# Output projection in seven block products: last sums made on chip, one operand split earlier, evictions and transposes in another order

## The chip, the core and the metric

The kernel runs on one core of a Trainium2 chip. Five engines work side by side, each through its own queue in order: TensorE (PE, with its weight loads shown apart as PEld), VectorE (DVE), ScalarE (ACT), GpSimd (POOL) and SyncE (SP), which issues the transfers. They meet at semaphores. The metric is the device time of one execution in microseconds; before the change the median of three runs is 1611.94 us (1611.52 to 1611.96).

## What is computed

One decoder block on a sequence of 1024 rows of 1024 features, all in float32. The part that matters here lies between the two branches and the feed-forward layer:

```python
branch_a = (jax.nn.silu(rg) * ry) @ w_ret_out[l]
branch_b = ay.reshape(B, S, ATTN_Q) @ w_attn_out[l]
merged = jax.nn.sigmoid(gate_a) * branch_a + jax.nn.sigmoid(gate_b) * branch_b
x = x + merged @ w_out[l]
h2 = rms_norm(x, ln2_g[l])
x = x + (jax.nn.silu(h2 @ w_ffn_gate[l]) * (h2 @ w_ffn_up[l])) @ w_ffn_down[l]
return rms_norm(x, lnf_g)
```

## The kernel before

**Numbers in two parts.** A float32 operand is split into a high part (a cast on ACT) and a low part (a subtraction on DVE); a product is three matmuls: high by high, high by low, low by high. `halves`, `wsplit` and `sum_halves` (L1301) make such pairs.

**Seven products.** The output projection `merged @ w_out` is cut into two by two blocks of 512 and done with seven block products, P1 to P7, in place of eight (Strassen's scheme in Winograd's form). `merged` is kept transposed; its blocks are a11, a21 (first and second half of the sequence, features 0 to 511) and a12, a22 (features 512 to 1023), those of w_out b11, b12, b21, b22. P1 takes a11 and b11, P2 a12 and b21. The others take sums: on the left S1 = a21 + a22 (P5), S2 = S1 - a11 (P6), a12 - S2 (P3), S3 = a11 - a21 (P7) and a22 alone (P4); on the right b12 - b11 (P5), t2 = b22 - (b12 - b11) (P6), b22 (P3), b22 - b12 (P7) and b21 - t2 (P4). Each product is 4 x 4 x 3 = 48 matmuls: four k of 128 features, four row tiles tt, three pairs.

**Branch A** (the loop over n, L1099) multiplies 128 features of branch A at a time, in the order 0, 4, 1, 5, 2, 6, 3, 7, each in two halves of the sequence of 24 matmuls, into three accumulator banks in turn. `evac` adds branch B and splits a11, a12 and a22 into m0 and m1. After each second n, k = n - 4 has all four blocks, and POOL makes the four sums of that k in place (L1120 to L1126) and SP writes them to DRAM (`ms_d`). From there P5's, P6's and P7's sums are read back whole (`load_sum`, L1296), then cast and subtracted (`sum_halves`).

**Tiles.** m0 and m1 hold four operand parts each; the tiles `wob` (b12, b22, t2) and `sA` (operands of P5 and P6) take the space of branch A's input, which its last product frees. x2 is the residual; it takes the space of branch A's temporaries, so its loads (`load_x`, L1299) wait for the last write to DRAM. `xf` and `a1` later take the space of `wob` and `sA`. P1, P6, P7 and P4 add up in the four banks `vbank`, P2, then P5 and P3 in the four banks `obank`, which have the names s and t.

**Order.** From L1366 DVE, ACT and PE are held to the written order (`in_order`); POOL's and SP's order is the scheduler's. `by_k` runs a product k by k over all row tiles, `by_t` one row tile with all k. `gain` (L1351) adds a bank into x2. The written order is P2, P1, P5, P6 by k, then P3 by row tile, then for each row tile of the second half P7 and P4, each followed by its `gain`. For each block t of 128 rows, `ln2_a` squares x2 and sums it (ACT, L1358), POOL makes the reciprocal root (L98, L100), `ln2_b` scales (ACT, L1362), and `columns` (L1224) transposes the result in eight matmuls and multiplies by the gain vector (L1237). For the first half `columns` also splits it into `a1` for the feed-forward products; for the second half it makes the Strassen sums (L1246 to L1248, on POOL for t below 6, else on DVE), which `s2_part` and `a22_part` split into m0 and m1. There are two tiles `hx` for the scaled blocks. `prep_to` splits feed-forward weights, `early_t` makes their sums.

## Time and profile before

| what | us |
|---|---|
| median of three runs | 1611.94 |
| the profiled execution | 1604.04 |
| its span, first to last instruction | 1602.2 |
| PE busy in the span | 1563.7 |
| DVE, ACT, POOL busy | 1020.0, 730.7, 406.4 |
| branch A's last matmul group ends, P2 starts | 850.73 |
| first feed-forward matmul starts | 965.90 |

Times inside the span count from its start. In the timeline a row merges instructions that follow each other without a gap: start, length, engine, line, operation, output<-inputs, count, and in brackets how long the engine had stood idle before and what ended that. Matmuls are pipelined, so their listed lengths overlap; the distance from start to start is what one takes.

### The profile page before, as it was taken

To read this page: it belongs to the slowest core of one execution; us is meant where nothing else is said; L and a number is where in the kernel's file an instruction comes from. 1 tells how busy PE (TensorE), PEld (TensorE's weight loads), DVE (VectorE), ACT (ScalarE), POOL (GpSimd) and SP (SyncE) were. 2 spreads that over 40 slices of the span, in tenths; PEclk is the share of its full clock that TensorE was granted. 3 is DMA by queue.
4 is the path that set the end of the run, shared out by engine and by line. 5 is a ranking of instruction groups with operands and counts; after the bars stand their busy time and mean duration, and the time that the engine had idled before them with its cause. 6 is when DMAs were issued, how large, how long until landed. Compare 5 with 4: busy or idle time off the path is not lost.

```text
span 1602.2 us, 20889 instructions
## 1 busy us (share of the span) xinstructions
PE 1563.7 (98%) x7435; PEld 1298.7 (81%) x7435; DVE 1020.0 (64%) x1792; ACT 730.7 (46%) x1456; POOL 406.4 (25%) x333
## 2 busy tenths in 40 slices
PE   9999999999999999999998969999999999999998
PEld 8887788888888888888886748888888888888886
DVE  6469987778566654887555658444444444578756
...
GB/s 210 167 155 145 178 216 165 108 138 39 186 171 152 132 158 238 209 195 113 219 184 259 93 1 59 99 106 99 106 105 108 114 100 102 277 258 92 99 99 125
DMA packets 154230, 231.51 MB, mean 144 GB/s; under 512 B 9420, under 2 KB 81934, under 8 KB 152591
## 3 DMA queue, kind: packets, MB, share of 16 engines
...
q8 instruction: 58, 0.95, 0.2%
q14 instruction: 46, 0.37, 0.1%
q10 hardware_dynamic: 2, 0.00, 0.0%
...
## 4 chain that ended last, share of the span: by engine, by line
PE 83%; ACT 6%; DVE 4%; issue 2%; DMA 2%; POOL 1%; SPq 0%; POOLq 0%; DVEq 0%; ACTq 0%
PE fA L1474 15%; PE fB L1474 7%; PE dA L1753 7%; PE wA L842 6%; PE dxP L1753 6%; PE fC L1474 4%; PE wB L842 3%; PE va L687 3%; PE acc_g L158 2%; PE acc_g L159 2%; PE acc_g L160 2%; PE vP L687 2%; ACT sc L467 2%; PE acc_bb L158 2%; PE acc_bb L159 2%
## 5 line engine op out<-in xcount | busy, mean ns | idle before, releaser
L1753 PE MATMUL dA<-dwP,daP 128*128 128x512 f32 x528 | 120.6, 389 | 0.0
L1753 PEld LDWEIGHTS dA<-dwP,daP 128*128 128x128 f32 x528 | 99.0, 188 | 20.7 <-DVE dwP L134 0.2
L1753 PE MATMUL dxP<-dwP,daP 128*128 128x512 f32 x396 | 90.2, 389 | 0.0
L1753 PEld LDWEIGHTS dxP<-dwP,daP 128*128 128x128 f32 x396 | 74.3, 188 | 15.4
L452 POOL COPY sc<-nsink 128x4 f32<-128x4 f32 x32 | 13.1, 412 | 274.4 <-PE pT L485 157.1
L158 PE MATMUL acc_g<-h,wh_g 128*128 128x512 f32 x192 | 75.5, 393 | 0.1
L159 PE MATMUL acc_g<-h,wh_g 128*128 128x512 f32 x192 | 75.2, 392 | 0.0
L160 PE MATMUL acc_g<-h,wl_g 128*128 128x512 f32 x192 | 75.1, 393 | 0.0
L467 ACT ACTIVATE sc<-sc,nm 128x257 f32<-128x257 f32 (+1 forms) x128 | 62.5, 492 | 27.1 <-DVE nm L464 26.7
L1543 POOL TENSOR_TENSOR xf<-xf 128x512 f32<-128x512 f32 x40 | 60.3, 1507 | 30.4 <-issue 28.8
L1485 POOL TENSOR_TENSOR xf<-xf 128x512 f32<-128x512 f32 x33 | 49.8, 1510 | 55.0 <-ACT t_1P L131 23.1
L464 DVE CUSTOM_DVE_ANT_0 sc<-s,amask,nsink 128x256 f32<-128x256 f32 (+1 forms) x128 | 54.2, 463 | 9.8 <-PE s L461 9.5
L1495 ACT COPY xf<-fA 128x512 f32<-128x512 f32 x44 | 25.7, 586 | 74.1 <-PE fA L1474 74.1
L1658 POOL TENSOR_TENSOR rs_f<-tot,mhalf 128x1 f32<-128x1 f32 x8 | 4.8, 605 | 205.4 <-DVE tot L1655 205.4
L134 DVE TENSOR_TENSOR dwP<-wd,dwP 128x512 fp32r<-128x512 f32 x77 | 52.9, 687 | 5.4 <-ACT dwP L131 5.4
L556 POOL TENSOR_TENSOR wr_wp<-wr_wp 128x512 f32<-128x512 f32 x10 | 16.6, 1657 | 140.0 <-DVE w0P L134 122.5
L131 ACT CAST dwP<-wd 128x512 fp32r<-128x512 f32 x77 | 47.4, 616 | 9.3 <-PE dA L1753 7.1
L158 PE MATMUL acc_bb<-ay,wh_bb 128*128 128x512 f32 x128 | 51.0, 400 | 0.0
L131 ACT CAST daP<-daP 128x512 fp32r<-128x512 f32 x42 | 26.0, 620 | 54.1 <-PE dxP L1753 26.7
L159 PE MATMUL acc_bb<-ay,wh_bb 128*128 128x512 f32 x128 | 50.3, 393 | 0.0
L160 PE MATMUL aq<-h,wl_aq 128*128 128x512 f32 x128 | 50.2, 392 | 0.0
L158 PE MATMUL aq<-h,wh_aq 128*128 128x512 f32 x128 | 50.2, 392 | 0.0
...
## 6 DMA issues: line engine op xcount, KB each, us to landing
...
daP<-act_d SPq DMA_DIRECT2D x21, 512.0 KB, 10.5
...
```

The source lines that it names most:

```text
L131: nc.scalar.copy(hi, raw)
L134: return nc.vector.tensor_tensor(out=lo, in0=raw, in1=f32(hi), op=ALU.subtract)
L158: nc.tensor.matmul(pt, hi[:, k, :], xh, start=(k == 0), stop=False)
L159: nc.tensor.matmul(pt, hi[:, k, :], xl, start=False, stop=False)
L160: nc.tensor.matmul(pt, lo[:, k, :], xh, start=False, stop=(k == 7))
L464: nc.vector.tensor_tensor_reduce(out=sc[:, j, 0:nk], in0=pt[:, jj * 256:jj * 256 + nk], in1=mk, scale=1.0, scalar=nsink[:, 4 * g + j:4 * g ...
L467: nc.scalar.activation(sc[:, j, 0:nk + 1], sc[:, j, 0:nk + 1], AF.Exp, scale=-1.0, bias=nm[:, j:j + 1], accum_out=den[:, j:j + 1])
L687: nc.tensor.matmul(vbanks[pr][tt], x_[:, c], w[:, u, :], start=(fresh and k + z == 0), stop=(k == 3 and z == 2), skip_group_check=not fresh)
L842: nc.tensor.matmul(pt, o[:, w, k, :], v, start=(first and k + z == 0), stop=(k == 3 and z == 2), skip_group_check=not first)
L1474: nc.tensor.matmul(pt, o[:, w, k, :], v, start=(first and k + z == 0), stop=(k == 3 and z == 2), skip_group_check=not first)
L1543: nc.gpsimd.tensor_tensor(out=o, in0=a, in1=b, op=op)
L1753: nc.tensor.matmul(banks[tt], a[:, u, c], w[:, v, :], start=(fresh and f + z == 0), stop=(f == NP - 1 and z == 2), skip_group_check=not fresh)
```

## The change

1. In branch A, for k = 0, 1, 2, S3 (P7's operand) is split into m1 at once (`halves`) and not written to DRAM.
2. For k = 3 the four sums are made on DVE, and ACT and DVE split three of them straight into `sA` and m1. Only P3's sum (a12) is written. `sA` is loaded for k below 3 only, and these loads and those of `wob` are issued ahead of it.
3. The helpers and the loads of b11 and b21 stand earlier in the text, and the written order on DVE and ACT begins there.
4. P5's weights are split ahead of the `gain` of P2, P6's sums and weights ahead of the `gain` of P1; t2 takes the place of b21 for P4, made on POOL after P6's split. `load(1)` comes before P3's weights.
5. Of the first half's blocks only two are squared and scaled inside P3. Then `c22(tt)` (P7 of a row tile and its `gain`) and `c21(tt)` (P4 and its `gain`) alternate with the columns: c22(0), c22(1), c21(0), c22(2), c21(1), c22(3), c21(2), c21(3). Column 6 comes between the first two feed-forward products, column 7 behind them.
6. `columns` no longer splits the first half; `hi_part` (ACT) and `lo_part` (DVE) do it later. S2's last two parts and all four of a22's stand behind column 7, and the transposes take s and t banks by turns.

```diff
-            if kh:
+            if kh and k < 3:
                 a11, a21, a12, a22 = (parts.pop(i) for i in ((0, 0), (0, 1), (1, 0), (1, 1)))
                 nc.gpsimd.tensor_tensor(out=a22, in0=a21, in1=a22, op=ALU.add)
                 nc.sync.dma_start(ms_d[0, k], a22)
                 nc.gpsimd.tensor_tensor(out=a21, in0=a11, in1=a21, op=ALU.subtract)
-                nc.sync.dma_start(ms_d[2, k], a21)
+                halves(a21, m1[:, 0, k, :], m1[:, 1, k, :])
...
+        for y in range(2):
+            nc.sync.dma_start(wob[:, 4 * y:4 * y + 4], blk(y, 1))
+            nc.sync.dma_start(f32(sA[:, 2 * y + 1, 0:3]), ms_d[y, 0:3].rearrange("k p t -> p k t"))
+
+        late = in_order(nc.vector.engine, nc.scalar.engine)
+        late.__enter__()
+        a11, a21, a12, a22 = (parts.pop(i) for i in ((0, 0), (0, 1), (1, 0), (1, 1)))
+        v_ = nc.vector.tensor_tensor
+        v_(out=a22, in0=a21, in1=a22, op=ALU.add)
+        v_(out=a21, in0=a11, in1=a21, op=ALU.subtract)
+        nc.scalar.copy(sA[:, 0, 3], a22)
+        v_(out=a11, in0=a22, in1=a11, op=ALU.subtract)
+        nc.scalar.copy(m1[:, 0, 3], a21)
+        v_(out=a12, in0=a12, in1=a11, op=ALU.subtract)
+        nc.scalar.copy(sA[:, 2, 3], a11)
+        nc.sync.dma_start(ms_d[2, 3], a12)
+        for hl, q, src in ((sA, 0, a22), (m1, 0, a21), (sA, 2, a11)):
+            v_(out=hl[:, q + 1, 3], in0=src, in1=f32(hl[:, q, 3]), op=ALU.subtract)
...
-            pt = ps("s", 2, f"h2T{t}{q}")
+            pt = ps("ts"[t % 2], 2, f"h2T{t}{q}")
...
     sub2(nc.vector, b11, b12, b11)
-    sum_halves("P5")
-    sum_halves("P7")
+    sum_halves("P5", 3)
     by_k("P2")
 
-    for tt in range(4):
-        gain(0, tt, 0, obank["P2"][tt])
     W["P5"] = slots4(("tw", "tw"), "P5")
     wsplit(b11, W["P5"])
     sub2(nc.gpsimd, t2, b22, b11)
+    for tt in range(4):
+        gain(0, tt, 0, obank["P2"][tt])
...
     for tt in range(4):
         by_t("P3", tt)
+        if 0 < tt < 3:
+            ln2_b(tt - 1)
         gain(0, tt, 1, obank["P5"][tt])
-        ln2_a(tt)
-        if tt > 1:
-            columns(tt - 2)
-        ln2_b(tt)
-    early_t(0, 2)
-    for tt in range(4):
-        t = 4 + tt
+        if tt < 2:
+            ln2_a(tt)
+        if tt == 2:
+            early_t(0, 2)
+
+    def c21(tt):
+        by_t("P4", tt)
+        gain(1, tt, 0, vbank[tt])
+
+    def c22(tt):
         by_t("P7", tt)
         gain(1, tt, 1, vbank[tt])
...
+    c22(3)
+    ln2_b(5)
+    columns(4)
+    prep_to(4)
+    c21(2)
+    ln2_a(6)
+    columns(5)
+    ln2_b(6)
+    c21(3)
+    ln2_a(7)
+    s2_part(4)
+    ln2_b(7)
```

Three places show how instructions move. The first is on DVE, from the end of branch A to P2's evictions. `woP1..` and `woP5..` are the weight halves of P1 and P5, `wr_b110` and `wrx_b111` the two halves of b11, `ms..` the four blocks of k = 3. Before:

```order
L1271 TENSOR_TENSOR woP111_8225<-wrx_b111_8206,woP110_8224 128x1024
L560 TENSOR_TENSOR m1_7577<-ms11_8181,m1_7577 128x512
L1275 TENSOR_TENSOR wr_b110_8205<-wob_8230,wr_b110_8205 128x1024
L1275 TENSOR_TENSOR wrx_b111_8206<-wob_8230,wrx_b111_8206 128x1024
L1307 TENSOR_TENSOR sA_8231<-sA_8231 128x1024 x2
L1307 TENSOR_TENSOR m1_7577<-m1_7577 128x1024 x2
L1351 SCALAR_TENSOR_TENSOR x2_8198<-woP20_8245,x2_8198 128x512
L1351 SCALAR_TENSOR_TENSOR x2_8198<-woP21_8246,x2_8198 128x512
L1351 SCALAR_TENSOR_TENSOR x2_8198<-woP22_8247,x2_8198 128x512
L1351 SCALAR_TENSOR_TENSOR x2_8198<-woP23_8248,x2_8198 128x512
L1271 TENSOR_TENSOR woP501_8312<-wr_b110_8205,woP500_8311 128x1024
L1271 TENSOR_TENSOR woP511_8314<-wrx_b111_8206,woP510_8313 128x1024
```
After the change the sums of k = 3 come in between, P7's halves leave, and P5's weights stand ahead of the evictions:

```order
L1183 TENSOR_TENSOR ms00_8078<-ms11_8184,ms00_8078 128x512
L1185 TENSOR_TENSOR ms10_8150<-ms10_8150,ms00_8078 128x512
L1189 TENSOR_TENSOR sA_8215<-ms11_8184,sA_8215 128x512
L1189 TENSOR_TENSOR m1_7577<-ms01_8112,m1_7577 128x512
L1189 TENSOR_TENSOR sA_8215<-ms00_8078,sA_8215 128x512
L1121 TENSOR_TENSOR wr_b110_8189<-wob_8214,wr_b110_8189 128x1024
L1121 TENSOR_TENSOR wrx_b111_8190<-wob_8214,wrx_b111_8190 128x1024
L1330 TENSOR_TENSOR sA_8215<-sA_8215 128x1024
L1330 TENSOR_TENSOR sA_8215<-sA_8215 128x512
L1117 TENSOR_TENSOR woP501_8309<-wr_b110_8189,woP500_8308 128x1024
L1117 TENSOR_TENSOR woP511_8311<-wrx_b111_8190,woP510_8310 128x1024
L1369 SCALAR_TENSOR_TENSOR x2_8235<-woP20_8250,x2_8235 128x512
```
The evictions (L1351, now L1369) moved from directly behind P7's halves to behind P5's weights. The first two of the four sums of k = 3 stand just ahead of this piece; its first two rows are the other two, the last of which is P3's.

The second is on POOL at the end of the norm: `ve_ln2_` and `rs_ln2_` with a block's number are its mean and the reciprocal root, `xf` the three sums of a column of the second half. After the change:

```order
L1295 TENSOR_TENSOR xf_8524<-xf_8524 128x4x128
L1296 TENSOR_TENSOR xf_8524<-xf_8524 128x4x128
L1297 TENSOR_TENSOR xf_8524<-xf_8524 128x4x128
L98 TENSOR_SCALAR ve_ln2_6_8820<-m2_8817 128x1
L100 TENSOR_TENSOR rs_ln2_6_8822<-ve_ln2_6_8820,mhalf_84 128x1
L1295 TENSOR_TENSOR xf_8524<-xf_8524 128x4x128
L1296 TENSOR_TENSOR xf_8524<-xf_8524 128x4x128
L1297 TENSOR_TENSOR xf_8524<-xf_8524 128x4x128
L98 TENSOR_SCALAR ve_ln2_7_8856<-m2_8853 128x1
L100 TENSOR_TENSOR rs_ln2_7_8858<-ve_ln2_7_8856,mhalf_84 128x1
```
Before, the same rows stand there in the same order, with L1246 to L1248 for L1295 to L1297: the sums of column 4, the root of block 6, the sums of column 5, the root of block 7. Nothing moved among them; what moved is the work of PE, DVE and ACT around them.

The third is on DVE, from the last evictions of the projection on (`t_0P1`, `t_0P2` are low parts of gate slab 0's P1 and P2 weights, `t_1..` of up slab 0's, `m0` here S2's low part, `wo..` a vbank). Before:

```order
L1351 SCALAR_TENSOR_TENSOR x2_8198<-wo2_8243,x2_8198 128x512 x2
L1237 TENSOR_TENSOR xf_8523<-h2T50_8800,bcol_87 128x4x128
L1237 TENSOR_TENSOR xf_8523<-h2T51_8806,bcol_87 128x4x128
L560 TENSOR_TENSOR m0_7576<-xf_8523,m0_7576 128x4x128
L560 TENSOR_TENSOR m1_7577<-xf_8523,m1_7577 128x4x128
L1351 SCALAR_TENSOR_TENSOR x2_8198<-wo3_8244,x2_8198 128x512
L134 TENSOR_TENSOR t_0P1_8845<-wr_f00_8321,t_0P1_8845 128x512
L134 TENSOR_TENSOR t_1P1_8848<-wr_f10_8518,t_1P1_8848 128x512
L1351 SCALAR_TENSOR_TENSOR x2_8198<-wo3_8244,x2_8198 128x512
```
After the change:

```order
L1369 SCALAR_TENSOR_TENSOR x2_8235<-wo3_8249,x2_8235 128x512
L1290 TENSOR_TENSOR xf_8524<-h2T40_8783,bcol_87 128x4x128
L1290 TENSOR_TENSOR xf_8524<-h2T41_8789,bcol_87 128x4x128
L134 TENSOR_TENSOR t_0P2_8798<-wrx_f01_8323,t_0P2_8798 128x512
L134 TENSOR_TENSOR t_1P2_8801<-wrx_f11_8392,t_1P2_8801 128x512
L1369 SCALAR_TENSOR_TENSOR x2_8235<-wo2_8248,x2_8235 128x512
L1290 TENSOR_TENSOR xf_8524<-h2T50_8824,bcol_87 128x4x128
L1290 TENSOR_TENSOR xf_8524<-h2T51_8830,bcol_87 128x4x128
L1369 SCALAR_TENSOR_TENSOR x2_8235<-wo3_8249,x2_8235 128x512
L560 TENSOR_TENSOR m0_7576<-xf_8524,m0_7576 128x4x128
```
Before, low parts of S2 and a22 and the P1 weight splits stood ahead of the last evictions of wo3. Now the P2 weight splits stand ahead of the last eviction of wo2 (the one that block 6 waits for), and the first low part of S2 stands behind the last eviction of wo3.

More of the change, by code (lines that the diff above doesn't have):

```diff
@@ L65, in hybrid_block @@
     rg_d = dram.tile([8, P, S], F32, name="rg_d")
-    ms_d = dram.tile([4, 4, P, 512], F32, name="ms_d")
+    ms_d = dram.tile([3, 4, P, 512], F32, name="ms_d")
     act_d = dram.tile([7, NF // 2, P, 512], F32, name="act_d")
@@ L1094, in hybrid_block, with slot, raw_pair, blk @@
     wdp = ctx.enter_context(tc.tile_pool(name="wdp", bufs=2, side="right"))
+    slots = {"wh": (ring, 2), "wl": (ring, 2), "tw": (wdp, 4)}
+    def slot(tag, shape, dt, name):
+        pool, bufs = slots[tag]
+        return pool.tile([P] + shape, dt, tag=tag, bufs=bufs, name=name)
+    def raw_pair(shape, name):
+        return [raw_slab(shape, name + "0"),
+                wdp.tile([P] + shape, F32, tag="wrx", bufs=2, name=f"wrx_{name}1")]
+    def blk(y, z):
+        return w_out[y * 512:y * 512 + 512, z * 512:z * 512 + 512].rearrange("(k p) n -> p k n", p=P)
+    def two(v, c):
+        return v[:, 2 * c:2 * c + 2]
+    def slots4(tags, name):
+        return [[slot(t_, [2, 512], F32R, f"wo{name}{c}{u}") for u, t_ in enumerate(tags)] for c in range(2)]
+    def wsplit(src, dst, eng=None):
+        for c in range(2):
+            nc.scalar.copy(dst[c][0], src[c])
+            (eng or nc.vector).tensor_tensor(out=dst[c][1], in0=src[c], in1=f32(dst[c][0]), op=ALU.subtract)
+    def sub2(eng, o, p, q):
+        for c in range(2):
+            eng.tensor_tensor(out=o[c], in0=p[c], in1=q[c], op=ALU.subtract)
     with tc.tile_pool(name="w3", bufs=1) as w3:
@@ L1126, in hybrid_block @@
                 nc.gpsimd.tensor_tensor(out=a12, in0=a12, in1=a11, op=ALU.subtract)
-                nc.sync.dma_start(ms_d[3, k], a12)
+                nc.sync.dma_start(ms_d[2, k], a12)
+        W = {}
+        with tc.high_priority(offset=AHEAD):
+            b11, b21 = raw_pair([2, 512], "b11"), raw_pair([2, 512], "b21")
+            for y, b in ((1, b21), (0, b11)):
+                for c in range(2):
+                    nc.sync.dma_start(b[c], two(blk(y, 0), c))
+            W["P2"] = slots4(("tw", "tw"), "P2")
+            wsplit(b21, W["P2"])
+            wdp.tile([P, 56], F32, name="pad_wdp", bufs=1)
+            W["P1"] = slots4(("wh", "wl"), "P1")
+            wsplit(b11, W["P1"])
@@ new lines, in hybrid_block @@
+        wob = act.tile([P, 16, 512], F32, tag="A", name="wob")
+        sA = act.tile([P, 4, 4, 512], F32R, tag="A", name="sA")
+        b12, b22, t2 = ([two(wob[:, 4 * i:4 * i + 4], c) for c in range(2)] for i in range(3))
+        for y in range(2):
[3 more added lines that the diff above has]
+        late.__enter__()
@@ L1237, in columns @@
             nc.vector.tensor_tensor(out=o, in0=pt.rearrange("p (k s) -> p k s", s=P), in1=g, op=ALU.mult)
-            if half == 0:
-                hi = a1[:, 2 * q, :, c]
-                nc.scalar.copy(hi, o)
-                nc.vector.tensor_tensor(out=a1[:, 2 * q + 1, :, c], in0=o, in1=f32(hi), op=ALU.subtract)
         if half:
@@ L1248, in columns, with hi_part, lo_part @@
             return eng.tensor_tensor(out=a12, in0=a12, in1=a11, op=ALU.subtract).ins
+    def hi_part(t):
+        c = slice(t * P, t * P + P)
+        for q in range(2):
+            nc.scalar.copy(a1[:, 2 * q, :, c], xf[:, q, :, c])
+    def lo_part(t):
+        c = slice(t * P, t * P + P)
+        for q in range(2):
+            nc.vector.tensor_tensor(out=a1[:, 2 * q + 1, :, c], in0=xf[:, q, :, c], in1=f32(a1[:, 2 * q, :, c]),
+                                    op=ALU.subtract)
     def s2_part(t):
@@ L1300, in load_x, with sum_halves @@
                           x[half * 512:half * 512 + 512, z * 512:z * 512 + 512].rearrange("(t p) n -> p t n", p=P))
-    def sum_halves(pr):
+    def sum_halves(pr, n):
         v, q = XA[pr]
-        for c in range(2):
-            hi, lo = two(v[:, q], c), two(v[:, q + 1], c)
+        for c in (slice(0, 2), slice(2, n)):
+            hi, lo = v[:, q, c], v[:, q + 1, c]
             nc.scalar.copy(hi, f32(lo))
@@ L1362, in ln2_b @@
         nc.scalar.activation(hxs[t], x2[:, t, :], AF.Copy, scale=lnr[t])
-    late = in_order(nc.vector.engine, nc.scalar.engine)
-    late.__enter__()
     first = in_order(nc.tensor.engine)
@@ L1579, in hybrid_block @@
         if i < 2:
+            if i:
+                columns(NB - 2)
+                s2_part(NB - 3)
             early.append((j, pr, multiply(j, pr)))
@@ L1606, in hybrid_block @@
             early_t(0, 4)
-            a22_part(NB - 2)
-            a22_part(NB - 1)
+            for t in range(4, NB):
+                a22_part(t)
             prep_to(11)
```

112 lines of the change are left out of this document (39 added, 73 removed).

## The prediction

> **What bounds the kernel now.** I read the head of the page first, then a window around the output projection, then TensorE's timeline there, then what it waited for.
>
> ```profile
> span 1602.2 us, 20889 instructions
> PE 1563.7 (98%) x7435; PEld 1298.7 (81%) x7435; DVE 1020.0 (64%) x1792; ACT 730.7 (46%) x1456; POOL 406.4 (25%) x333
> ...
> 850.70:977.80 127.10, 101.59 (x450) 82.09 (x449) 79.03 (x97) 53.29 (x77) 43.02 (x34) 0.92 0.29 105
> ```
> TensorE (PE) is busy for 98% of the span, so time can be won only where it stands still or runs slowly. The window from the projection's first matmul to (gate slab 0, P6), the first feed-forward product that needs all of the norm's output, is such a place: 127.10 us with 101.59 busy, at a granted clock of 0.92. The timeline of PE shows where (columns: start, length, line, out<-in, count, idle time before and its releaser):
>
> ```profile
> 850.73 11.04 PE L1334 MATMUL woP<-woP,m 128*128 128x512 f32 x48
> 861.61 11.04 PE L1334 MATMUL wo<-woP,m 128*128 128x512 f32 x48
> ...
> 880.31 0.76 PE L1334 MATMUL woP<-woP,sA 128*128 128x512 f32 x1 [7.66 <-DVE x L1351]
> 883.14 12.36 PE L1334 MATMUL woP<-woP,sA 128*128 128x512 f32 x47 [2.07 <-DVE woP L1271]
> ...
> 927.66 4.36 PE L1334 MATMUL wo<-m,m 128*128 128x512 f32 x12 [2.65 <-DVE x L1351]
> 931.86 1.04 PE L1229 MATMUL h2T<-ident,hx 128*128 128x128 f32 x8
> 932.65 3.02 PE L1334 MATMUL wo<-woP,m 128*128 128x512 f32 x12
> ...
> 939.13 3.02 PE L1334 MATMUL wo<-m,m 128*128 128x512 f32 x12 [3.46 <-DVE x L1351]
> ...
> 948.81 3.02 PE L1334 MATMUL wo<-m,m 128*128 128x512 f32 x12 [3.06 <-DVE x L1351]
> ...
> 960.17 5.10 PE L1334 MATMUL wo<-m,m 128*128 128x512 f32 x12 [4.73 <-DVE x L1351]
> ...
> 977.78 2.88 PE L1474 MATMUL fA<-m,t_0P 128*128 128x512 f32 x12
> ```
> Two batches of 48 matmuls start 861.61 - 850.73 = 10.88 us apart: 0.2267 us each, with nothing between. A column's eight transposes take 932.65 - 931.86 = 0.79. The window holds 7 x 48 projection matmuls, 4 x 12 of the feed-forward and 8 columns: 384 x 0.2267 + 8 x 0.79 = 93.4 us. It takes 977.78 - 850.73 = 127.05. So **33.7 us** are lost there, in two places. P5 should start at 861.61 + 10.88 = 872.5 and end 11.04 later at 883.5; it ends at 883.14 + 12.36 = 895.5, first late, then on a slow clock (12.36 for 47): 12.0 lost. The rest, 21.7, goes in P3, P7, P4 and the norm, where the four second-half blocks start (939.13 to 960.17, two intervals) 10.5 apart for work of 2 x 2.72 + 0.79 = 6.2.
>
> ```profile
> PE wo L1334 <- DVE x L1351: 13.9, 4, 4.7
> PE woP L1334 <- DVE x L1351: 7.7, 1, 7.7
> ```
> Both are waits for L1351, the eviction of a bank into x2 by VectorE (DVE). It waits in its engine's order, not for its bank. Before P5, what stands ahead of it waits on ScalarE (ACT):
>
> ```profile
> 867.56 2.01 ACT L1306 CAST sA<-sA 128x1024 fp32r<-128x1024 f32 x2 [14.57 <-DMA sA<-ms_d]
> 875.75 1.99 ACT L1306 CAST m<-m 128x1024 fp32r<-128x1024 f32 x2 [6.18 <-DMA m<-ms_d]
> ```
> ACT stands behind the sums that come back from DRAM: P5's at 867.56, P7's at 875.75.
>
> **The change part by part.** First, **the start of P5**. P7's reload, its two casts and two subtractions leave this place; P7's operand is made in branch A for k below 3. P5's and P6's sums of k = 3 never leave the chip. For P5 the old path was four POOL sums after branch A, a write, a read. The new one is on DVE:
>
> ```profile
> 852.26 1.22 DVE L1271 TENSOR_TENSOR woP<-wrx_b,woP 128x1024 fp32r<-128x1024 f32 x1
> 853.40 0.68 DVE L560 TENSOR_TENSOR m<-ms,m 128x512 fp32r<-128x512 f32 x1
> 854.00 1.22 DVE L1275 TENSOR_TENSOR wr_b<-wob,wr_b 128x1024 f32<-128x1024 f32 x1
> 855.14 2.31 DVE L1275 TENSOR_TENSOR wrx_b<-wob,wrx_b 128x1024 f32<-128x1024 f32 x1
> 868.65 6.49 DVE L1307 TENSOR_TENSOR sA<-sA 128x1024 fp32r<-128x1024 f32 x2 [11.20 <-ACT sA L1306]
> ```
> The split of P1's last weights (852.26) and the last half (853.40) stay. Then come four sums and three low parts of 512, seven at about 0.65 us (they are listed at 0.69 and start 0.60 to 0.72 apart), with ACT's three casts beside them: 854.0 to 858.4. The two subtractions for b11, 1.14 apart as at 854.00 and 855.14, end at 860.7. Are the loads there?
>
> ```profile
> 848.64 0.50 SPq L1314 DMA_DIRECT2D wob<-in_w_out  x1
> ...
> 861.78 0.37 SPq L1296 DMA_DIRECT2D sA<-ms_d  x1
> 863.64 0.38 SPq L1299 DMA_DIRECT2D x<-in_x  x1
> ```
> ```profile
> 848.00:852.00 4.00, 4.00 (x19) 3.32 (x18) 1.32 (x3) 1.05 (x1) 0.00 (x0) 1.00 0.59 208
> 852.00:856.00 4.00, 4.00 (x20) 3.30 (x19) 4.00 (x5) 0.62 (x1) 1.84 (x1) 1.00 0.82 316
> ```
> Both w_out loads started at 848.2 and 848.64, and 208 x 4 + 316 x 4 = 2.1 MB moved by 856, their size. Now the two sum loads (0.75 MB each) follow from 850.75, when the last product of branch A frees their tile. In all 3.7 MB at 316 GB/s and a little more: P5's sums at about 857, b22 at 859 to 860, the last at 861. x(0,0) went out at 863.64, when the last sum's write had landed, about 2.2 us after it; now a12's write goes out at 856.7 and x at 859. From 863.64 to the first use of x at 879.5 are 15.8 us, which bounds its landing by 875; a load of the same size, 861.78 to 867.56, took 5.8, and by that it lands at 865. I take 866, nearer to the second since less is queued with it.
>
> What decides is POOL, which starts on t2 and b12 (two operations each of 2.4 us) as b11 is ready:
>
> ```profile
> 854.16 2.21 POOL L1120 TENSOR_TENSOR ms<-ms,ms 128x512 f32<-128x512 f32 x1 [15.12 <-DVE m L560]
> 856.45 2.15 POOL L1122 TENSOR_TENSOR ms<-ms,ms 128x512 f32<-128x512 f32 x1
> 858.68 1.29 POOL L1124 TENSOR_TENSOR ms<-ms,ms 128x512 f32<-128x512 f32 x1
> ...
> 868.34 2.41 POOL L1275 TENSOR_TENSOR wrx_b<-wrx_b,wob 128x1024 f32<-128x1024 f32 x1
> 870.70 6.65 POOL L1275 TENSOR_TENSOR wob<-wob 128x1024 f32<-128x1024 f32 x2
> ```
> Beside DVE's two subtractions at 854.00 and 855.14 POOL's two took 2.21 and 2.15 instead of 1.29, and DVE's second 2.31. Laid end to end (1.14, 1.26, 1.14, 1.2) they fill the time exactly: the engines alternate. From 868.34 the three POOL operations (7.1) and two of DVE (2.3) end at 877.35, 9.0 us: the same. An operation of DVE that reads PSUM, as the evictions do, keeps its length beside POOL:
>
> ```profile
> 834.67 0.69 DVE L1111 SCALAR_TENSOR_TENSOR ms<-tar,acc_ba 128x512 f32<-128x512 f32 x1 [1.76 <-POOL ms L1120]
> ```
> So from 860.7 four POOL operations (9.5) alternate with DVE's two halves of P5's sums (1.14, 0.6) and two of its weights (2 x 1.14), 4.0 in all: DVE is through at 874.2, evicts P2's first bank, and P5 starts 0.8 later (879.49 to 880.31 before): **875.0, a wait of 2.5**. If both engines merely ran at half speed, DVE would be through at 868.7, the four evictions at 871.2, and the wait would be nothing. That is the other end. [...]
>
> After that P5 and P6 run to 875.0 + 21.8 = 896.8. P6's operands (DVE, about 881) and P1's evictions (883) come before its start at 885.9. P3's sums are loaded from 872.5, when P1 has read that buffer; even with the 14.0 us from the first sum load of before to P7's use (861.78 to 875.75) they are there at 886.5 and split by 891; P3 needs them at 896.8. P7's and P4's weights follow on tiles that P5 and P6 free. I cost all these at nothing: if P6 were late by 1 us, all behind it would be.
>
> In branch A the three new casts and subtractions (0.6 each) stand on DVE ahead of the next eviction and wait for POOL's second sum, 2.6 us into its four. For k = 2 that sum is ready at about 835.7, so the eviction of 834.67 comes at about 837.1. PE takes its three banks in turn and comes back to this one two halves of 5.44 later, at 845: covered, nothing. Of 16 writes to DRAM 10 remain.
>
> **Second, the order of P7, P4 and the norm.** Before, P4 of a block came 2.7 us after P7 of the same block and needed its eviction, which stood in DVE's order behind column work that waited on ACT. Now P7 of block 0 and P4 of block 0 are a P7 and two columns apart. A column's chain is:
>
> ```profile
> 942.18 0.69 DVE L1351 SCALAR_TENSOR_TENSOR x<-wo,x 128x512 f32<-128x512 f32 x1 [3.11 <-PE wo L1334]
> ```
> ```profile
> 942.91 1.06 ACT L1358 ACTIVATE hx<-x 128x1024 f32<-128x1024 f32 x1 [5.44 <-DVE x L1351]
> ...
> 945.05 1.15 ACT L1362 ACTIVATE hx<-x,rs_ln 128x1024 f32<-128x1024 f32 x1 [0.99 <-POOL rs_ln L100]
> ```
> ```profile
> 944.45 0.57 POOL L100 TENSOR_TENSOR rs_ln<-ve_ln,mhalf 128x1 f32<-128x1 f32 x1
> 944.98 1.28 POOL L1246 TENSOR_TENSOR xf<-xf 128x512 f32<-128x512 f32 x1
> ```
> Eviction at 942.18, squares at 942.91, POOL's root at 944.45, scaling from 945.05 to 946.2: 4.0 us, beside at least 6.2 us of PE's other work per column now. The splits into high and low (2 x 0.6 on ACT, 2 x 0.6 on DVE per column) moved behind, so ACT has 3.9 us per column of the first half. Followed block by block from P3 at 896.8, no step to column 5 waits: P3 ends 907.7, the last P4 but one at 930.7.
>
> **Third, the tail**, where the order on POOL and DVE is closest. POOL makes the sums of column 4, three of about 1.3 (944.98), from 929.3. DVE has the two P2 weight splits ahead of the eviction of block 6; each waits out a POOL operation (931.2, 933.1), so that eviction starts at 933.1, its scaling ends at 937.1, and PE, which reaches column 6 after eight twelves, six columns and one feed-forward product at 907.7 + 9 x 2.72 + 6 x 0.79 = 936.9, waits **0.2**. POOL then has the sums of column 5 ahead of block 7's root (936 to 940.4 with one DVE operation between); root 941.2, scaling 942.4. PE wants column 7 at 937.1 + 0.79 + 2.72 = 940.6: **1.8**. The two P2 products and the column last until 948.6. On ACT, column 6's scaled half stands behind that scaling:
>
> ```profile
> 972.53 1.14 ACT L1233 ACTIVATE xf<-h2T,bcol 128x128 f32<-128x128 f32 x4 [0.26 <-PE h2T L1229]
> ```
> So it ends at 943.5. From there DVE does eleven operations of 512 (three sums of column 6, a low part, column 7's eviction, its three sums, a low part, a weight split, the last low part of S2), 11 x 0.65 = 7.2: 950.7. PE wants S2 at 948.6: **2.2**. Behind that DVE is 2 us later against PE than before, and the four a22 splits now come together; I count **0.2** more at P7.
>
> The sum: 33.7 - (2.5 + 0.2 + 1.8 + 2.2 + 0.2) = **26.8 us** off. Unknown is the clock: after its wait of 2.65 the block at 927.66 took 4.36 for 2.85 to 3.02 elsewhere (1.4 more), after 3.46 and 3.06 none, after 4.73 5.10 (2.1 more). I take nothing for waits of 2.5 and less, with twice 1.4 as the other end. [...]
>
> The profiled execution took 1604.04 us (its span 1602.2) where the three runs shown have a median of 1611.94. 1604.04 - 26.8 = 1577.2; in the ratio of the two, 1.0049, that is 26.9 off the median: **1585.0 us**. Below 1578, all waits gone, nothing in this window can bring it.
>
> **The rivals.** *Everything hides*: b22 lands after DVE is through P5's weights, and the tail's chains are as short as the rows: 33.7 off, 1578. For it: a load 1.2 us later than I put it is enough for the first part. Against: the tail hangs on orders, not on landing. *The column waits move to the second half*: blocks 4 to 7 wait on DVE and POOL as they do now, 10.5 - 6.2 = 4.3 each, 17.2 in place of my 4.2: 1598. For it: POOL's sums and DVE's exclusion fall there. Against: each eviction has 3.5 us more cover. *Slower than before*: all eight columns lose it. The place is the norm's chain through the in-order queues and its two hx buffers; eight waits of 4.3 and P5's 2.5 are 36.9, so 3.2 more than now: 1615. It decides at (33.7 - 2.5) / 8 = 3.9 us per column, a chain of about 10 us for the measured 4.0. *It doesn't do what it says*: sums on chip still come late because P5 hangs on x alone; with 875 for its landing P5 starts at 875.8, no more than 0.8 on top, inside the forecast's range.
>
> **How the numbers follow.** Forecast 0.63 (its own range 1581 to 1590), all hidden 0.18, second-half waits 0.13, slower 0.03, gains given back behind the projection until nothing is left 0.03 (against it: from the second pair of slabs on every engine has the same rows in the same order as before). Within 0.2% (3.2 us), about what a measurement of this kernel can tell from no change, is only the last. The range from 1578 to 1594 takes in the first two, the clock's end (2.8) and a P6 late by some us; it leaves out about 0.19. Faster 0.94, same 0.03, slower 0.03.
>
> **What would show it.** P5's first matmul 24 to 25 us after P2's, with DVE's P5 weight subtractions at about twice their length and POOL between them, shows the first step right; at 21.8 the exclusion was hidden. No wait for L1369 above 0.5 us before column 6, then waits of 1 to 3 us at columns 6 and 7 and the first P6, show the second and third. The window from P2's first matmul to (0, P6) should be about 100 us. Wrong would be a wait before P6 or P3 of the projection, a clock below 0.95 in the window, or a loss behind it.

## The result, and the profile after

The changed kernel takes **1582.46 us** (median of 4 runs, 1581.99 to 1583.26) where the kernel before takes 1611.73 beside it (4 runs, 1610.33 to 1611.96): the ratio is 0.9821, 95% interval 0.9804 to 0.9838. The forecast was 1585.0, range 1578 to 1594. The profiled execution took 1582.22, and from the head of its page, and from a table of the window from P2's first matmul to (gate slab 0, P6):

```profile
span 1580.4 us, 20869 instructions
PE 1560.8 (99%) x7435; PEld 1297.5 (82%) x7435; DVE 1024.5 (65%) x1800; ACT 732.3 (46%) x1460; POOL 404.0 (26%) x329
```
```profile
853.28:953.85 100.57, 95.61 (x450) 78.53 (x448) 84.04 (x97) 51.10 (x75) 39.15 (x30) 1.00 0.31 110
```
The window took 127.05 us before at a granted clock of 0.92; now it takes 100.57 at 1.00 (101.59 busy in it before, 95.61 now). It ends here at the second matmul of (0, P6), the one that waits; the first ran alone at 951.97, after 98.69 us. TensorE's timeline shows where it still stands (start, length, line, out<-in, count, idle time before and its releaser):

```profile
853.28 11.04 PE L1352 MATMUL woP<-woP,m 128*128 128x512 f32 x48
...
877.20 11.14 PE L1352 MATMUL woP<-woP,sA 128*128 128x512 f32 x48 [2.00 <-DVE x L1369]
888.18 11.04 PE L1352 MATMUL wo<-m,sA 128*128 128x512 f32 x48
...
910.89 0.65 PE L1282 MATMUL h2T<-ident,hx 128*128 128x128 f32 x4 [0.35 <-DVE x L1369]
...
945.39 1.09 PE L1282 MATMUL h2T<-ident,hx 128*128 128x128 f32 x8 [1.24 <-ACT hx L1380]
...
953.85 2.83 PE L1512 MATMUL fA<-m,t_0P 128*128 128x512 f32 x11 [1.38 <-DVE m L560]
...
966.61 3.01 PE L1512 MATMUL fA<-m,t_0P 128*128 128x512 f32 x12 [1.77 <-ACT xf L1533]
```
Five waits are left: 2.00 before P5, 0.35 in column 0, 1.24 before column 7, 1.38 in (0, P6), 1.77 before (0, P7). P6 and P3 of the projection start without one, and so does column 6.

To compare runs, I take the stretch from P2's first matmul to the first matmul of slab 2, 1002.26 - 850.73 = 151.53 before and 980.34 - 853.28 = 127.06 after. By the prediction's floor (93.4 up to (0, P6), then nine blocks of 12 at 2.72) it would take 117.9 without any loss. What is above that splits into the waits that TensorE's rows name and the rest, which is mostly matmuls that ran slowly (about 1.7 us of it is there at a granted clock of 1.00 too, in all_three). In the table these three are of each run's profiled execution. Behind the stretch nothing differs: from slab 2 to the end of the span are 599.94 us before and 600.06 after. What differs in front of it, 850.73 against 853.28 for P2's start, comes from the first 14 us of the program, in which, for one, four small matmuls took 2.25 us in the one execution and 3.78 in the other. It falls either way for any kernel here (P2 starts between 850.7 and 853.5).

| run | us, median (range, runs) | ratio to before, 95% | stretch | waits | rest |
|---|---|---|---|---|---|
| before | 1611.73 (1610.33 to 1611.96, 4) | | 151.53 | 25.5 | 8.1 |
| before_again | 1609.58 (1606.90 to 1611.88, 10) | 0.9993 (0.9983 to 1.0002) | 155.87 | 25.5 | 12.5 |
| sums_only | 1600.52 (1599.63 to 1602.04, 4) | 0.994 (0.9926 to 0.9953) | 146.28 | 17.6 | 10.8 |
| order_only | 1591.75 (1590.26 to 1592.38, 4) | 0.9883 (0.9869 to 0.9896) | 137.47 | 14.5 | 5.1 |
| after | 1582.46 (1581.99 to 1583.26, 4) | 0.9821 (0.9804 to 0.9838) | 127.06 | 6.7 | 2.4 |
| after_again | 1582.00 (1579.94 to 1583.19, 5) | 0.9821 (0.9801 to 0.984) | 130.26 | 6.8 | 5.6 |
| b12_late | 1579.53 (1577.71 to 1579.72, 5) | 0.9806 (0.9793 to 0.9819) | 124.83 | 4.8 | 2.1 |
| pool_writes | 1579.63 (one run) | | 126.44 | 4.8 | 3.8 |
| col5_dve | 1581.27 (1580.61 to 1582.25, 4) | 0.9823 (0.9804 to 0.9842) | 126.62 | 5.2 | 3.5 |
| a22_early | 1580.70 (1578.97 to 1581.04, 4) | 0.9817 (0.9798 to 0.9836) | 125.62 | 5.3 | 2.5 |
| one_bank | 1581.28 (1580.03 to 1581.46, 4) | 0.9821 (0.9806 to 0.9835) | 126.47 | 6.5 | 2.1 |
| pairs | 1584.03 (1582.64 to 1584.51, 4) | 0.9836 (0.982 to 0.9853) | 129.34 | 8.2 | 3.3 |
| splits_in | 1581.01 (1580.05 to 1585.25, 4) | 0.9826 (0.9809 to 0.9843) | 127.04 | 6.7 | 2.4 |
| all_three | 1575.61 (1574.73 to 1576.30, 4) | 0.9787 (0.9768 to 0.9806) | 121.22 | 1.6 | 1.7 |

The waits repeat from execution to execution (25.5 and 25.5 in the two profiles of before, 6.7 and 6.8 in the two of the changed kernel), the rest does not (8.1 and 12.5, 2.4 and 5.6). That is the key to most of what follows.

### The profile page after: what moved, and what is told of

Same layout as the page of the kernel before. It is cut to its first block, busy times and chain, and to the rows that moved or that the text cites. A ratio compares the mean times of both kernels' runs of the same rounds, so it can differ in the third digit from the quotient of the medians.

```text
span 1580.4 us, 20869 instructions
## 1 busy us (share of the span) xinstructions
PE 1560.8 (99%) x7435; PEld 1297.5 (82%) x7435; DVE 1024.5 (65%) x1800; ACT 732.3 (46%) x1460; POOL 404.0 (26%) x329
## 4 chain that ended last, share of the span: by engine, by line
PE 86%; ACT 6%; DVE 6%; issue 2%; POOL 1%; POOLq 0%; DVEq 0%; ACTq 0%
PE fA L1512 14%; PE fB L1512 7%; PE dA L1797 7%; PE wA L842 7%; PE dxP L1797 6%; PE fC L1512 3%; PE wB L842 3%; PE va L687 3%; PE acc_g L158 2%; ACT sc L467 2%; PE vP L687 2%; PE acc_g L159 2%; PE acc_g L160 2%; PE acc_ba L159 2%; PE acc_ba L158 2%; PE acc_ba L160 2%
## 5 line engine op out<-in xcount | busy, mean ns | idle before, releaser
L1533 ACT COPY xf<-fA 128x512 f32<-128x512 f32 x44 | 25.9, 588 | 75.1 <-PE fA L1512 75.1
L556 POOL TENSOR_TENSOR wr_f<-wr_f 128x512 f32<-128x512 f32 x20 | 30.7, 1535 | 76.8 <-DVE t_14P L134 8.6
```

## The experiments

**Two halves.** Two kernels make half of the change each, beside a second look at the kernel before.

before_again: the kernel before, unchanged.

> The kernel before, profiled once more; nothing is changed. Open: its profile took 1604.04 us where its timed runs took 1611.7, so the profiles of before and after differ by 21.8 us of span, the timed runs by 29.3. Theory A (the clock): in most executions the matmuls behind the long wait at P5 run longer at the lower clock, so a profile near 1611 would show the 7 to 8 us as slow matmuls inside the projection's window (granted clock there below 0.90, window 130 to 135 us instead of 127). Theory B: the 7 to 8 us lie elsewhere (at the start or in the feed-forward part), and the window stays at 127 us.

sums_only takes the last sums on the chip, the early split of S3 and the new order up to P3, and leaves the order of P7, P4 and the norm as before. Against the changed kernel, cut:

```diff
-            pt = ps("ts"[t % 2], 2, f"h2T{t}{q}")
+            pt = ps("s", 2, f"h2T{t}{q}")
...
-    columns(0)
-    ln2_a(2)
-    hi_part(0)
-    c22(0)
...
+    for tt in range(4):
+        t = 4 + tt
+        by_t("P7", tt)
+        gain(1, tt, 1, vbank[tt])
...
```

> Part 1 alone: sums of k = 3 on chip, P7's operand in branch A, P5's weights ahead of P2's evictions; P3, P7, P4 and the norm in the old order. My theory (two separate places): P5 starts about 24 us after P2 (32.4 before), the window's later part loses what it lost before (about 21 us), so 10 us less than before in the profile and 1598 to 1602 timed. Rival (one resource): the old order behind P5 is late because P5 is late, so starting P5 early wins most of the 29 us: below 1590. Rival (nothing without the order): the time won at P5 is waited away at P7 and P4: 1608 or more.

order_only is the other half: the new order of P7, P4, the norm and the splits, with the sums through DRAM and the order up to P3 as before. Against the changed kernel, cut:

```diff
-            if kh and k < 3:
+            if kh:
...
-                halves(a21, m1[:, 0, k, :], m1[:, 1, k, :])
+                nc.sync.dma_start(ms_d[2, k], a21)
...
-    sum_halves("P5", 3)
+    sum_halves("P5")
+    sum_halves("P7")
```

> Part 2 alone: the new order of P7, P4, the norm and its columns, with all sums still written to DRAM and read back and P2's evictions where they were. My theory: P5 still starts about 30 us after P2 and runs slowly at first (12 us lost), P3 to the first P6 of the feed-forward loses 3 to 6 us instead of 21.7, so about 15 to 17 us less than before in the profile, 1594 to 1598 timed; the two parts alone add up to the whole within 3 us. Rival: the parts hang on each other (P7's or P4's operands come too late for the new order), and this gains less than 8 us: 1604 or more.

Rows of TensorE in before_again; they answer to the four blocks in the prediction's rows of before:

```profile
929.54 4.52 PE L1334 MATMUL wo<-m,m 128*128 128x512 f32 x12 [2.65 <-DVE x L1351]
...
941.16 5.45 PE L1334 MATMUL wo<-m,m 128*128 128x512 f32 x12 [3.50 <-DVE x L1351]
...
953.29 4.59 PE L1334 MATMUL wo<-m,m 128*128 128x512 f32 x12 [3.04 <-DVE x L1351]
...
966.22 4.92 PE L1334 MATMUL wo<-m,m 128*128 128x512 f32 x12 [4.72 <-DVE x L1351]
```
The waits are those of the first profile (2.65, 3.46, 3.06, 4.73). But there two of the four blocks ran at full rate behind theirs, 3.02 us, and here none does: 5.45 and 4.59. This execution took 1609.89, the first 1604.04; 4.3 us of the difference lie in the stretch and all of them in its "rest", 1.5 in the start. The window up to (0, P6) takes 131.39 us, as the first theory had it, and the mean granted clock over the whole span is 0.988 for 0.993 in the first profile, but only 0.4 of the 4.3 us fall behind the wait at P5, on which it had put them; 4.0 fall in the four blocks. So the profile of before on which the prediction rests came from an execution that lost little clock behind its waits; all ten timings of before_again lie above it, 1606.90 to 1611.88.

What TensorE waits for in sums_only (in all, times, longest), then in order_only:

```profile
PE wo L1356 <- DVE x L1373: 13.7, 4, 4.7
PE h2T L1282 <- DVE xf L1290: 2.0, 2, 1.2
PE woP L1356 <- DVE x L1373: 2.0, 1, 2.0
```
```profile
PE woP L1341 <- DVE x L1358: 7.7, 1, 7.7
PE woP L1341 <- DVE woP L1278: 2.1, 1, 2.1
...
```
Each half removes its own waits and leaves the other's where they were: 7.7 + 2.1 become 2.0 with the sums, 13.7 and 2.0 are gone with the order. Against the kernel before in the same comparison (1611.18) they win 10.7 and 19.4 us, 30.1 together, where the whole change wins 29.3: the halves add. sums_only came out inside its expectation; order_only is 2 us better than the 1594 to 1598 expected of it, since with the four waits much of the slow clock behind them went too (its rest is 5.1, against 8.1 and 12.5 in the two profiles of before).

**The start of P5.** b12_late takes POOL's two operations for b12 away from P5's weight subtractions and puts them behind t2's:

```diff
     load(0)
     sum_halves("P6", 3)
-    sub2(nc.gpsimd, b12, b22, b12)
...
-    sub2(nc.gpsimd, t2, b21, t2)
+    with in_order(nc.gpsimd.engine):
+        sub2(nc.gpsimd, t2, b21, t2)
+        sub2(nc.gpsimd, b12, b22, b12)
```

> The changed kernel with POOL's two subtractions for b12 (P7's weights) held behind those for P4's weights: nothing else moves. My theory (DVE and POOL take turns while both read two operands from SBUF): only two POOL operations remain beside DVE's five before P2's evictions, DVE is through 4.5 to 5 us earlier (872 instead of 876.4 by the profile of after), P5 starts at once, 21.8 us after P2 instead of 23.9: about 2 us less than the changed kernel, 1580.5. Rival (DVE is slowed by the transfers that run at the same time, not by POOL): DVE's operations keep their 3.4 us and P5 its wait; no change, 1582.5.

In the changed kernel DVE and then POOL, from the second half of b11 to the eviction for which P5 waits:

```profile
863.53 6.24 DVE L1330 TENSOR_TENSOR sA<-sA 128x1024 fp32r<-128x1024 f32 x2
869.70 3.42 DVE L1117 TENSOR_TENSOR woP<-wr_b,woP 128x1024 fp32r<-128x1024 f32 x1
873.04 3.42 DVE L1117 TENSOR_TENSOR woP<-wrx_b,woP 128x1024 fp32r<-128x1024 f32 x1
```
```profile
865.83 3.39 POOL L1121 TENSOR_TENSOR wob<-wob 128x1024 f32<-128x1024 f32 x1
869.18 2.84 POOL L1121 TENSOR_TENSOR wob<-wob,wrx_b 128x1024 f32<-128x1024 f32 x1
871.99 3.38 POOL L1121 TENSOR_TENSOR wob<-wob 128x1024 f32<-128x1024 f32 x1
```
And in b12_late, DVE at the same place and P5's first matmul:

```profile
867.40 1.21 DVE L1117 TENSOR_TENSOR woP<-wr_b,woP 128x1024 fp32r<-128x1024 f32 x1
868.54 1.21 DVE L1117 TENSOR_TENSOR woP<-wrx_b,woP 128x1024 fp32r<-128x1024 f32 x1
```
```profile
872.74 11.04 PE L1352 MATMUL woP<-woP,sA 128*128 128x512 f32 x48
```
The same subtraction takes 1.21 us with POOL idle and 3.42 beside one of POOL's, and POOL's take 2.8 to 3.4 beside it: about the 1.2 and the 2.4 of the two alone (POOL's by the prediction's row at 868.34), one after the other. The transfers are not what slows DVE: in the changed kernel they ran at 396 GB/s while its subtraction at 861.26 (L1121, 128x1024), with POOL idle, took 1.22 us, and at 407 beside the two long ones. P5 now starts without a wait, and the median is 1579.53 us (1580.5 was expected); no timing of it reaches one of the changed kernel's in either of its two measurements. That also settles the rival by which P5 hangs on the load of x: the load is there by 869.67, when the eviction begins in this kernel, right behind the second of these subtractions.

pool_writes asks which work of POOL does this. It is b12_late with four writes of zeros by POOL into a part of `wob` that nothing reads, at the time of these subtractions:

```diff
-    sub2(nc.gpsimd, t2, b22, b11)
+    with in_order(nc.gpsimd.engine):
+        sub2(nc.gpsimd, t2, b22, b11)
+        for c in range(4):
+            nc.gpsimd.memset(wob[:, 12 + c % 2 * 2:14 + c % 2 * 2], 0.0)
```

> b12_late with four POOL writes of zeros (128x1024 each, into a part of wob that nothing reads) behind t2's two subtractions, so that they run while DVE does P5's two weight subtractions (1.21 us each in b12_late, where POOL is idle beside them, 3.42 in the changed kernel beside POOL's subtractions). If any work of POOL on SBUF shuts DVE out, these two take over 2 us again and a wait before P5 may come back. If only a POOL instruction that also reads SBUF does, they stay at 1.2 and P5 starts without a wait.

POOL and DVE in pool_writes:

```profile
863.81 3.39 POOL L1121 TENSOR_TENSOR wob<-wob,wrx_b 128x1024 f32<-128x1024 f32 x1
867.14 3.65 POOL L1395 MEMSET wob<- 128x1024 f32 x4
```
```profile
861.51 6.24 DVE L1330 TENSOR_TENSOR sA<-sA 128x1024 fp32r<-128x1024 f32 x2
867.67 1.21 DVE L1117 TENSOR_TENSOR woP<-wr_b,woP 128x1024 fp32r<-128x1024 f32 x1
```
Beside writes DVE keeps its 1.21; beside POOL's subtraction at 863.81 its two halves take 6.24 for 2.3. In these rows only POOL's work that also reads shuts it out.

**The tail.** Three places are left there. after_again is the changed kernel once more, as their measure.

> The changed kernel once more, beside the three below. Theory and rival agree on 1582 to 1584 us; it gives the waits of a second profile: P5 2.0, column 7 1.2, first gate product of P6 1.4, first of P7 1.8. If these four are set by the order of the queues they come back within 0.2 us; if by landings or by the clock they scatter by more.

col5_dve moves the three sums of column 5 from POOL to DVE (their code is put into a function `sums`, cut here):

```diff
-            eng = nc.gpsimd if t < 6 else nc.vector
+            eng = nc.gpsimd if t < 5 else nc.vector
...
     c21(3)
+    sums(5)
     ln2_a(7)
```

> The three sums of column 5 go from POOL to DVE, behind c21(3). Theory: POOL's sums stand ahead of block 7's root, so without them the root comes about 3 us earlier; column 7's wait of 1.2 is gone, that of the first P6 (1.4) shrinks to about 0.9 since DVE has 2.1 us more to do in front of it, time 1.5 to 2 us less than the changed kernel's in the same call. Rival: DVE is the tail's bound; its three sums push the eviction of block 7 or the last low parts back, the wait moves to P6 and the time is the same or up to 1 us more.

a22_early moves only the four casts of a22 on ACT:

```diff
             pieces(xf[:, 2], m1[:, 2], m1[:, 3])
             prep_to(8)
+            for t in range(4, NB):
+                c = slice(t % 4 * P, t % 4 * P + P)
+                nc.scalar.copy(m1[:, 0, :, c], xf[:, 3, :, c])
...
             for t in range(4, NB):
-                a22_part(t)
+                c = slice(t % 4 * P, t % 4 * P + P)
+                nc.vector.tensor_tensor(out=m1[:, 1, :, c], in0=xf[:, 3, :, c], in1=f32(m1[:, 0, :, c]),
+                                        op=ALU.subtract)
```

> Only the four casts of a22 on ACT move, ahead of the casts of P5's operand, into a stretch of 3.9 us in which ACT waits for DVE; their subtractions on DVE stay. Theory: the wait of 1.8 before the first gate product of P7 is ACT's queue: the copy that frees the bank stands behind these four casts (2.2 us). It falls to 0.3 or less, time 1.4 to 1.8 us less than the changed kernel's. Rival: P7's own operand, whose last low part DVE ends at 964.2, or the weights' subtraction right behind it at 964.8, is as late as the bank; then 0.5 us or less is won.

all_three joins b12_late, col5_dve and a22_early.

> b12 made late as in b12_late, the sums of column 5 on DVE and the early casts of a22. If the three waits are independent the gains add: 2.9 + 1.5 to 2 + 1.4 to 1.8, so 1576 to 1577.5 us, with at most 1.5 us of waiting left between P2 and the first gate product of P7 against 9.1 in the changed kernel. If one covers another (the casts hidden behind a later tail, say), it stays above 1578.

Two rows of TensorE in after_again, then the granted clock (third number from the end) in the 3.5 us behind the same waits, first of after_again, then of after:

```profile
874.99 12.72 PE L1352 MATMUL woP<-woP,sA 128*128 128x512 f32 x48 [2.01 <-DVE x L1369]
...
965.96 4.49 PE L1512 MATMUL fA<-m,t_0P 128*128 128x512 f32 x12 [1.77 <-ACT xf L1533]
```
```profile
874.90:878.40 3.50, 3.41 (x8) 2.77 (x9) 3.50 (x6) 0.00 (x0) 0.00 (x0) 0.52 0.88 254
...
965.90:969.40 3.50, 3.44 (x11) 2.71 (x12) 3.50 (x7) 1.53 (x4) 0.00 (x0) 0.68 0.81 281
```
```profile
877.20:880.70 3.50, 3.50 (x15) 2.89 (x16) 3.50 (x6) 0.00 (x0) 0.00 (x0) 1.00 0.97 278
966.60:970.10 3.50, 3.49 (x15) 2.92 (x16) 3.50 (x7) 1.87 (x4) 0.00 (x0) 1.00 0.77 269
```
The four large waits came back within 0.01 us (the fifth, in column 0, is 0.34 for 0.35), so the order of the queues sets them. But behind two of them the clock was 0.52 and 0.68 here and 1.00 there, 1.6 and 1.5 us apiece.

For column 7, POOL and ACT in the changed kernel:

```profile
941.58 1.29 POOL L1297 TENSOR_TENSOR xf<-xf 128x512 f32<-128x512 f32 x1
...
943.58 0.57 POOL L100 TENSOR_TENSOR rs_ln<-ve_ln,mhalf 128x1 f32<-128x1 f32 x1
```
```profile
944.19 1.15 ACT L1380 ACTIVATE hx<-x,rs_ln 128x1024 f32<-128x1024 f32 x1 [2.58 <-POOL rs_ln L100]
```
and TensorE's waits in col5_dve:

```profile
PE woP L1356 <- DVE x L1373: 2.0, 1, 2.0
PE fA L1517 <- ACT xf L1538: 1.8, 1, 1.8
PE fA L1517 <- DVE m L560: 1.1, 1, 1.1
...
```
With the sums off POOL, its root comes when ACT has the squares, the wait at column 7 is gone and that of (0, P6) shrinks from 1.4 to 1.1: 1.6 us of waiting less, as the theory had it. In time this is 0.7 us (1581.27 for 1582.00), inside both runs' scatter: the profiled execution lost 1.4 of it again behind the wait at (0, P7), where its block took 4.37 us. So the mechanism is shown, the gain in time by itself is not.

For (0, P7), ACT in the changed kernel, then in a22_early:

```profile
963.38 2.17 ACT L559 CAST m<-xf 128x512 fp32r<-128x512 f32 x4
...
965.99 0.56 ACT L1533 COPY xf<-fA 128x512 f32<-128x512 f32 x1
```
```profile
954.15 2.18 ACT L1646 CAST m<-xf 128x512 fp32r<-128x512 f32 x4
...
961.84 1.05 ACT L1533 COPY xf<-fA 128x512 f32<-128x512 f32 x2
```
(0, P7) adds into the bank that the copy of L1533 reads; that result, (0, P6)'s, was there at 953.85 + 2.83 = 956.7, and the copy came at 965.99, because the four casts and what they stand behind came first in ACT's order. With the casts in a stretch in which ACT waits for DVE anyway, the copy ends before P7 needs the bank: that wait is gone and 0.26 appear at (1, P4). Waits fall by 1.5 us, the median by 1.3 (1580.70 for 1582.00, just under the 1.4 to 1.8 expected); the ranges of the two overlap, so here too the wait is shown and the gain in time by itself is not.

What all_three still waits for:

```profile
PE fA L1518 <- DVE m L560: 1.1, 1, 1.1
PE h2T L1282 <- DVE x L1373: 0.3, 1, 0.3
PE fA L1518 <- ACT xf L1539: 0.2, 1, 0.2
```
The gains in waits add (2.0, 1.6 and 1.5 make 5.1; 6.8 became 1.6). In time it is 6.4 us below the changed kernel measured beside it, 1575.61 for 1582.00, and no run of the one reaches a run of the other. It is 1.3 us more than the waits, and the "rest" is the smallest of all runs, 1.7, at a granted clock of 1.00: with the waits the slow clock behind them seems to go too. So it lies a little below the 1576 to 1577.5 expected. (The 9.1 us that the expectation calls waiting in the changed kernel are its waits and its rest together, 6.7 and 2.4.) It beats both kernels.

**Which part of the new order counts.** Three kernels undo one part of it each, measured beside each other. one_bank lets all transposes take the two s banks again:

```diff
-            pt = ps("ts"[t % 2], 2, f"h2T{t}{q}")
+            pt = ps("s", 2, f"h2T{t}{q}")
```

> The changed kernel, but all transposes take the two s banks, as before, in place of s and t by turns. Theory: nothing (within 0.5 us), since the bank that column t writes was read by DVE for column t-1 some 6 us earlier; only the wait of 0.3 at column 0, whose bank is still to be evicted, may change. Rival: column t's transposes wait for the multiplication of column t-1 in the tail, where DVE is late, up to 1 us at columns 6 and 7.

pairs puts P4 of a block back behind P7 of the same block, in the slots of the new order:

```diff
     lo_part(0)
-    c22(1)
+    c21(0)
...
     lo_part(1)
-    c21(0)
+    c22(1)
...
     early_t(1, 2)
-    c22(2)
+    c21(1)
```

> The changed kernel, but P4 of a block follows P7 of the same block in the next slot: c22(0), c21(0), c22(1), c21(1) and so on; columns, splits and the rest stay in their slots, so that one column (0.8 us) or nothing stands between the two. P4 adds into the bank that P7's eviction reads. Theory: what cost time before was the eviction's place in DVE's order, behind column work that waits for ACT; here it stands ahead of that, so P4 waits only for the eviction itself (about 1.0 us from P7's last matmul, less the column): 0.3 us where a column lies between, 1 us where none does, 1.5 to 4 us in all: 1583.5 to 1586. Rival: the distance of two products and two columns is what removed the waits; then 2.5 to 3.5 us come back at each of the four blocks and the time is 1592 to 1596.

splits_in makes the high and low parts right behind their column again:

```diff
     columns(1)
+    hi_part(1)
+    lo_part(1)
     ln2_a(3)
-    hi_part(1)
-    lo_part(0)
     c22(1)
```

> The changed kernel, but the high and low parts of columns 0 to 3 are made right behind their column on ACT and DVE, as before. Theory: ACT then stands in its queue until DVE has multiplied the column, so the squares of the next block start about 2.5 us later; the cover is 6.2 - 4.0 = 2.2 us per column, so each of the columns 1 to 3 waits between 0 and 1 us: 0 to 3 us on the changed kernel. Rival: the late splits are what opened the chain; then columns 1 to 4 wait 2 us and more, 8 us or more in all.

one_bank has the 1.2 at column 7 as before, a wait of 0.4 inside that column, where the second bank is still being read by ACT, and 0.3 less each at column 0 and (0, P6): nothing in all (1581.28). splits_in has the waits of the changed kernel to 0.01 us and its time within the scatter (1581.01): ACT does stand 2.3 us for column 0's multiplication, but the squares of block 2 still come in time. In pairs:

```profile
922.50 3.06 PE L1352 MATMUL wo<-m,m 128*128 128x512 f32 x12 [0.79 <-DVE x L1369]
...
930.65 3.02 PE L1352 MATMUL wo<-m,m 128*128 128x512 f32 x12 [1.48 <-DVE x L1369]
...
938.55 3.02 PE L1352 MATMUL wo<-m,m 128*128 128x512 f32 x12 [0.39 <-DVE x L1369]
```
P4 of block 0 does not wait, the others wait 0.79, 1.48 and 0.39; the wait at column 7 goes in exchange, and the time is 2.8 and 3.0 us above the two runs beside it, as the theory had it, and not the 10 or more of the rival. So P4 close behind P7 brings back 2.7 of the 13.9 us of the four waits, and the first half's splits right behind their columns bring back nothing. The kernel before had both at once, and sums_only, which has its whole order, has 13.7 of these waits. What stood ahead of the evictions is seen on DVE in the kernel before:

```profile
936.45 0.69 DVE L1241 TENSOR_TENSOR a<-xf,a 128x512 fp32r<-128x512 f32 x1 [0.68 <-ACT a L1240]
...
938.39 0.68 DVE L1351 SCALAR_TENSOR_TENSOR x<-wo,x 128x512 f32<-128x512 f32 x1
942.18 0.69 DVE L1351 SCALAR_TENSOR_TENSOR x<-wo,x 128x512 f32<-128x512 f32 x1 [3.11 <-PE wo L1334]
...
946.74 1.41 DVE L560 TENSOR_TENSOR m<-xf,m 128x512 fp32r<-128x512 f32 x1 [2.67 <-ACT m L559]
948.07 0.68 DVE L1351 SCALAR_TENSOR_TENSOR x<-wo,x 128x512 f32<-128x512 f32 x1
951.87 0.69 DVE L1351 SCALAR_TENSOR_TENSOR x<-wo,x 128x512 f32<-128x512 f32 x1 [3.12 <-PE wo L1334]
```
In the third of the four blocks the chain is this. The eviction of the second block's P4 (942.18) starts the squares, the root and the scaling; a22's cast stands behind the scaling on ACT; a22's low part waits for the cast at 946.74; and P7's eviction of the third block, long possible, stands behind that at 948.07. Only then does P4 of that block run, and its eviction is at 951.87. That is a ring of 951.87 - 942.18 = 9.7 us per block for 6.2 us of TensorE's work. In the second block P7's eviction (938.39) stands in the same way behind a column of the first half, whose low parts (the last at 936.45) each wait for a cast on ACT. The other two blocks are alike: P7's eviction of the first (926.92) stands behind a first-half low part at 924.98, that of the last (959.44) behind the second-half low parts at 956.85. So the first two waits (2.65 and 3.46) stand behind the first half's splits and the last two (3.06 and 4.73) behind the second half's. The new order takes both kinds away from these evictions and also sets P4 apart from P7. That the whole of it removes the waits is shown by order_only. How much each part would do alone is shown only so far as pairs and splits_in go: no run has the first half's splits and the close pair together, and none puts the second half's splits back, so that these splits ahead of a close pair make the waits is argued from the rows.

## Why the prediction was right

**The start of P5** went as forecast: the operations of DVE and POOL took turns whole, P5 starts 23.92 us after P2 (forecast 24 to 25), a wait of 2.0 for 2.5, with DVE's weight subtractions at 2.8 times their length (3.42 us for 1.21, forecast about twice); sums_only shows it alone and b12_late takes it away. The other end, half speed for both, would have shown no wait.

**The order of P7, P4 and the norm**: no wait from P6 of the projection to column 6, except the 0.35 in column 0, which was not forecast; its bank is evicted just then. The forecast gave two reasons, the eviction's place in DVE's order behind column work that waits on ACT, and more cover between P7 and P4. The rows of before show the first. pairs shows that the cover by itself is worth 2.7 us of waits, not 13.9; it does not show how much it adds where the splits stand ahead of the eviction.

**The tail**: forecast 0.2 at column 6, 1.8 at column 7, 2.2 at (0, P6) and 0.2 at (0, P7); measured 0, 1.24, 1.38 and 1.77. Column 6 comes without a wait, where the signs to look for had named 1 to 3 us there too. Column 7 and (0, P6) are right in mechanism (col5_dve, and DVE's low part named in the row at 953.85) and forecast somewhat too long. The fourth is the step that was mis-sized: "the four a22 splits now come together; I count 0.2 more at P7" looked at DVE being late, where the wait is ACT's copy behind those casts, and cost 1.77. The sum of all waits, 6.9 forecast and 6.74 measured, agrees because these errors cancel.

**The clock** was the second one: "I take nothing for waits of 2.5 and less" was the author's estimate, and none of the four blocks of the first profile stood behind a wait that short (2.65 to 4.73). One execution of the changed kernel bears it out (rest 2.4, of which about 1.7 is not clock), the other lost 3.2 us more behind waits of 2.0 and 1.8, which is 0.4 beyond the other end, 2 x 1.4.

**From the profiled execution to the median**: the forecast scaled 26.8 by 1.0049 and took 26.9 off; 29.3 came off (28.0 against the runs beside after_again). Two errors of opposite sign stand behind that. Between the two profiled executions the stretch lost 151.53 - 127.06 = 24.5 us, so the sum was 2.3 too large there: it put the rest at nothing. And the profile of before was a lucky one: by before_again an execution nearer to the median has the same waits and loses 4.3 us more in the stretch, behind them, and that part goes with the waits, while the ratio of 1.0049 gave it 0.1. Worked out afterwards, 33.7 + 4.3 lost, less 6.9 of waits, less some 3 of clock behind them, would have been 28. That the forecast lies as near as 2.5 us to the median is in part luck.

**The rivals** did not come: all hidden is nearly reached by b12_late and the two fixes in the tail together (1.6 us of waits left), and at 1575.6 it lies below the 1578 under which the prediction saw nothing that could bring the time, for the reason just given (the slow clock that went with the waits); waits in the second half were 4.4 us and not 17; the norm's chain never became the bound; P5 did not hang on x.
